# Layer 1's attention probabilities: turned in pairs through block transposes and a DRAM scratch, beside wider weight splits, scaling on ScalarE and smaller buffers

## The chip, the core and the metric

The program runs on one core of a Trainium2 chip. Time is the device time of one execution in microseconds (us), and what is compared is the median of several runs. The engines named below are TensorE (PE in the profile, with its weight loads as PEld), VectorE (DVE), ScalarE (ACT), GpSimd (POOL) and SyncE (SP, which here issues DMAs).

## The reference, cut to what matters

Two decoder layers on 256 tokens of width 2048, batch 1, all in float32. Layer 0 mixes tokens by block-sparse attention, which for 256 keys in one block is causal attention with 16 heads of 128; layer 1 by multi-head latent attention. Each is followed by a gated MLP of width 5632 with a causal convolution. The change is in layer 1's attention, and the order of a few small operations in layer 0 goes with it:

```python
def mla_attention(h, pos, wq_a, g_qa, wq_b, wkv_a, g_kva, wkv_b, g_qn, g_kn, g_qr, g_kr, wo):
    cq = rms_norm(h @ wq_a, g_qa)
    q = (cq @ wq_b).reshape(B, S, H, NOPE + RD)          # 16 heads, 128 + 64
    q_nope = rms_norm(q[..., :NOPE], g_qn)
    q_rope = rope(rms_norm(q[..., NOPE:], g_qr), pos, RD)
    kv_a = h @ wkv_a
    ckv = rms_norm(kv_a[..., :MLA_KV_RANK], g_kva)
    k_rope = rope(rms_norm(kv_a[..., MLA_KV_RANK:], g_kr)[:, :, None, :], pos, RD)[:, :, 0]
    kv = (ckv @ wkv_b).reshape(B, S, H, NOPE + VD)
    k_nope = rms_norm(kv[..., :NOPE], g_kn)
    v = kv[..., NOPE:]
    def block(i, qn, qr):                                # 128 queries
        s = (einsum('bqhd,bkhd->bhqk', qn, k_nope) + einsum('bqhr,bkr->bhqk', qr, k_rope)) * scale
        s = where(pos[None, :] <= q_pos[:, None], s, NEG_INF)
        p = softmax(s, axis=-1)
        return einsum('bhqk,bkhd->bqhd', p, v)
    o = sweep_query_blocks(block, (q_nope, q_rope), Q_BLOCK)
    return o.reshape(B, S, H * VD) @ wo
```

## The kernel before

All weights stream from HBM once. They come in **pieces** of 128 x 512 float32 (16 pieces of 128 x 576 for `mla_wkv_a`), two pieces to a **unit** of 512 KB, 740 units in all. `Stream.load` starts a unit's DMA on SyncE's queue into one of `AHEAD_UNITS` = 6 raw buffers. `Stream.split` (L113) turns a piece w into two float32r parts: ScalarE copies `whi` (rounded), VectorE subtracts to get `wlo` = w - whi. Each product of TensorE is made of three: hi x hi, hi x lo, lo x hi. The two parts of a piece stand in one of 5 buffers of a pool; a piece is split up to 4 pieces before its use.

The work of TensorE is a list `quanta`, one entry for each piece: `tok_major` (6 products with 512 moving columns, the activations as weights) or `feat_major` (12 products with 256 moving columns, the piece as weights). The loop at the end of `trunk` (L1343) writes out, for each quantum q, `ws.split(q + 4)`, then the quantum's products, then what was planned for q: `first_in` entries (`leading`) ahead of `at` entries (`side`). So every engine's program is in the order of the quanta, and a number such as q0 + 9 in a plan is a place in that order, not a time.

Layer 0's attention works in groups g of four heads, 48 quanta each; two heads form a `Pair` (L665): their scores are made, exponentiated and normalised in one tile `s` of 6 x 128 columns; `cross` (L677) turns 32 x 32 blocks on VectorE and writes them to DRAM with four DMAs, `crossed` (L681) reads them back with one, and `turned` (L684) splits what arrived into hi and lo parts. `values` then multiplies by v, and `parted` splits the output into `oT`.

Layer 1's attention has 12 quanta to a group (four pieces each of keys, queries and values; group 0 has four more for the rotary part). A head (class `Head`, L548) is on its own: `scores` (L555), `biased` (mask and row minimum, VectorE), `exps` (ScalarE), `normal` (L614, one reciprocal and two multiplications on VectorE), `turn` (L619, three 128 x 128 transposes on TensorE into PSUM), `turned` (L625, two copies on ScalarE and a subtraction on VectorE), `values` (L634) and `parted` (L645). Head i of a group has its scores at q0 = q_q + 11 + 3i, its transposes at q0 + 6 and its values at q0 + 9 (8 for the fourth), where q_q is the group's last quantum of queries (in group 0, of keys). A group's transposes, values and scores of three different heads so fall in one quantum. Two PSUM banks (`ps_sc`) serve scores and outputs in turn, two (`ps_tp`) the transposes, four the accumulators.

At the start, `Stream.begin` (L94) issues the first six units and x in alternation. `n1.sums` (quantum 29) needs the sum of 16 squares, one VectorE addition each (L346) in quanta 17 to 28; `signed_gains` (L816, 6 small VectorE operations) stands at quantum 26 and `gained_moba` (L827, 3 each) at 27 and 28.

Of the kernel before, what the change touches and what calls it, by code (L numbers as in the profile page):

```python
# [41 lines left out]

AHEAD_UNITS = 6
AHEAD_PIECES = 4

SINGLE_UNITS = 8
# [23 lines left out]
class Stream:  # L70

    def __init__(self, nc, raw_pool, part_pool, units, starts):
        self.starts = starts
# [18 lines left out]
    def begin(self, load_x):  # L94

        ends = {1: 3, 3: 5, 5: 8, 8: 12, 11: 16}
        load_x(0, 1)
        at = 1  # L100
        for u in range(AHEAD_UNITS):
            src, k, n = self.units[u]
            self.raw[u] = t = self.raw_pool.tile([P, 2 * 512], F32, name="raw")
            for i in range(k):
                queue = self.nc.scalar if u == i == 0 else self.nc.sync
                queue.dma_start(t[:, i * n : (i + 1) * n], src[:, i * n : (i + 1) * n])
                end = ends.get(u * k + i, at)
                if end > at:
                    load_x(at, end)
                    at = end  # L110
        self.loaded = AHEAD_UNITS

    def split(self, upto):  # L113
        while self.split_to < min(upto, len(self.pieces)):
            i = self.split_to
            u, j, n = self.pieces[i]
            self.load(u + AHEAD_UNITS)
            w = self.raw[u][:, j * n : (j + 1) * n]
            b, c = self.starts(u, j)
            hi = self.part_pool.tile([P, 512 + ROOM], F32R, name="whi")[:, b : b + max(n, 512)]  # L120
            lo = self.part_pool.tile([P, 512 + ROOM], F32R, name="wlo")[:, c : c + max(n, 512)]
            if i == 0:
                self.nc.vector.tensor_copy(hi[:, :n], w)
            else:
                self.nc.scalar.copy(hi[:, :n], w)  # L125
            self.nc.vector.tensor_tensor(  # L126
                lo[:, :n], w, hi[:, :n].bitcast(F32), op=ALU.subtract
            )
            self.parts[i] = (hi, lo, n)
            self.split_to += 1  # L130

# [5 lines left out]
def trunk(ctx: ExitStack, tc: tile.TileContext, a, out):  # L137
# [33 lines left out]
    units += grouped("mla_wqr", 1, 0)  # L171
    units += units_of("mla_wkv_a", 2 * KVN)
    for g in range(4):
        names = ("mla_wkn", "mla_wqn", "mla_wv") if g else ("mla_wqn", "mla_wqr", "mla_wkn", "mla_wv")
        for name in names:
            units += grouped(name, 1, 1 if name == "mla_wqr" else g)
    units += units_of("mla_wo")
    units += units_of("ffn_gu1")
# [7 lines left out]
    assert len(units) == 740  # L186
    ws = Stream(nc, raw_pool, part_pool, units, starts)

# [8 lines left out]

    zeros = const.tile([P, 512], BF16, name="zeros")
    nc.vector.memset(zeros, 0.0)
# [221 lines left out]
    class Heads:  # L421
# [22 lines left out]
        def squared(self, t):  # L444

            if self.gain is not None:
                if t == 0:
                    self.blk = att_pool.tile([P, NT, 4 * P], F32, name="blk", bufs=1)
                sq = self.blk[:, t]
            else:  # L450
                sq = att_pool.tile([P, 16 * 32], F32, name="sq" if self.dh == P else "ro2", bufs=2)
            nc.scalar.activation(sq, self.x[:, t].rearrange("p n d -> p (n d)"), AF.Square)
# [35 lines left out]
        def rotate(self, t, stages=range(4)):  # L488
# [11 lines left out]
            def part(name):  # L500
                r = att_pool.tile([P, n * rot], F32, name=name, bufs=2)
                return r.rearrange("p (n r) -> p n r", n=n)
# [45 lines left out]
    class Head:  # L548
# [34 lines left out]
        def biased(self):  # L583
            if self.pair:
                self.s_first, self.s_second = self.pair.scores_of(self.i % 2)
            else:
                self.s = att_pool.tile([P, 3 * P], F32, name="s", bufs=3)
                self.s_first, self.s_second = self.s[:, :P], self.s[:, P:]
# [25 lines left out]
        def normal(self):  # L614
            nc.vector.reciprocal(self.st[:, 4:6], self.st[:, 2:4])
            for k, x in enumerate((self.s_first, self.s_second)):
                nc.vector.tensor_scalar(x, x, self.st[:, 4 + k : 5 + k], None, op0=ALU.mult)

# [6 lines left out]
        def turned(self):  # L625

            pT = att_pool.tile([P, 2, S], F32R, name="pT", bufs=2)
            self.pT1 = att_pool.tile([P, P], F32, name="pT1", bufs=2)
            self.pT = hi, lo = pT[:, 0], pT[:, 1]
# [3 lines left out]

        def values(self):  # L634
            o = ps_sc.tile([P, 512], F32, name="sc")
            if self.pair:
                self.pT, self.pT1 = self.pair.turned_of(self.i % 2)
            v = self.v()
            vs = slice(self.i * P, (self.i + 1) * P)
            v0, v1 = v  # L640
            three(o[:, :S], v0[:, 0, vs], v0[:, 1, vs], self.pT[0], self.pT[1], True, False)
            mm(o[:, P:S], v1[:, vs], self.pT1, start=False, stop=True)  # L642
            self.o = o
# [21 lines left out]
    class Pair:  # L665
# [31 lines left out]

        def plan(self, heads, q, q_values):
            for hd in heads:
                at(q, hd.scores)  # L700
                at(q, hd.biased)
            for hd in heads:
                at(q + 1, hd.exps)
            for hd in heads:
                at(q + 2, hd.normal)
            at(q + 3, self.cross)
            at(q + 5, self.crossed)
            first_in(q_values - 2, 1, self.turned)
            for hd in heads:
                first_in(q_values, 0, hd.values)  # L710
                first_in(q_values, 0, hd.parted)

# [338 lines left out]
    def kva_squares(half):  # L1051
# [4 lines left out]
        for t in range(NT):  # L1056
            for k, lo, hi in cols:
                junk = att_pool.tile([P, 512], F32, name="kvjunk", tag="ro1", bufs=2)
                nc.vector.tensor_tensor_reduce(
# [238 lines left out]
    for g in range(4):  # L1298
        for kind in "kqv" if g else "qrkv":
# [10 lines left out]
            else:  # L1310
# [10 lines left out]
                plan_latent(q, hs, ("qT" if kind == "q" else "kT", g), with_gain(put, c), *steps)  # L1321
        for i in range(4):
            hd = Head(
                4 * g + i, lambda g=g: env["qT", g], lambda g=g: env["kT", g], lambda g=g: env["v", g],
                i, lambda: env["oT"],
                rope=lambda h=4 * (g % 2) + 2 * (i % 2) + i // 2: (env["qrT"][:, h], env["kr"]),
            )
            q0 = q_q + 11 + 3 * i
            last = g == i == 3
            hd.plan(q0, q0 + (7 if last else 8 if i == 3 else 9), q0 + 5 if last else None)  # L1330

# [132 lines left out]
```

## Time and profile before

| | us |
|---|---|
| median of 3 runs | 2073.11 (2072.75 to 2073.43) |
| the profiled execution: its own time | 2073.38 |
| the profiled execution: span, first to last instruction | 2071.1 |
| TensorE busy in the span | 2065.1 |
| VectorE busy | 1420.7 |
| ScalarE busy | 1157.7 |
| mean granted TensorE clock | 1.000 of full speed |

The span is what the profile's views divide up; 2.3 us of the execution lie around it. Matmuls are pipelined, so the duration of one (about 276 ns for 256 columns) is longer than the distance from its start to the next one's start; costs on TensorE are read from starts. VectorE's and ScalarE's instructions overlap their neighbours by a little as well, so that sums of durations come out above busy time.

### The profile page before, as it was taken

What the parts mean: (1) busy time and instruction counts of PE and PEld (TensorE: products, weight loads), DVE (VectorE), ACT (ScalarE), POOL (GpSimd) and SP (SyncE); (2) the same over time, 40 slices, a digit from 0 to 9 for tenths busy, and PEclk for the clock granted to TensorE, in tenths of its full rate; (3) what the DMA queues carried; (4) which work ended last, traced back from release to release, by engine and by line L of the source; (5) the groups of instructions that cost most, each with busy time, mean ns of one, the idle gap of its engine ahead of it and who ended that gap; (6) DMA issues with size and microseconds to landing.
All of it is one profiled execution on the core that took longest, in us unless ns stands there. A gap on an engine that the chain in (4) does not pass through costs nothing.

```text
span 2071.1 us, 42736 instructions
## 1 busy us (share of the span) xinstructions
PE 2065.1 (100%) x16630; PEld 1999.5 (97%) x16630; DVE 1420.7 (69%) x2781; ACT 1157.7 (56%) x2244; POOL 47.1 (2%) x38
## 2 busy tenths in 40 slices
PE   9999999999999999999999999999999999999999
PEld 7888899999999999999999889999999999999999
DVE  7877777766676666655556897767666766665554
ACT  6656666555555555555555786655555555544443
POOL 0000000000000000000000110000000000000000
PEclk9999999999999999999999999999999999999999
DMA  7777776555555555555554533555555555556563
GB/s 272 234 246 224 231 233 208 194 193 195 194 196 192 194 195 196 197 196 192 194 196 154 193 128 131 196 189 192 194 194 198 191 194 194 198 201 200 196 212 123
DMA packets 123931, 406.47 MB, mean 196 GB/s; under 512 B 14528, under 2 KB 25280, under 8 KB 123728
## 3 DMA queue, kind: packets, MB, share of 16 engines
q1 hardware_dynamic: 123408, 403.38, 58.0%
q8 instruction: 130, 2.13, 0.4%
q14 instruction: 73, 0.60, 0.1%
q10 hardware_dynamic: 288, 0.33, 0.1%
q0 software_dynamic: 32, 0.04, 0.0%
HBM read 394.25 MB, written 9.44 MB: 195 GB/s over the span
## 4 chain that ended last, share of the span: by engine, by line
PE 98%; DVE 1%; DMA 1%; ACT 0%; issue 0%; SPq 0%; DVEq 0%; ACTq 0%
PE acc L301 26%; PE acc L303 26%; PE acc L302 26%; PE acc L275 16%; PE tp L536 0%; PE sc L544 0%; PE sc L545 0%; PE sc L543 0%; PE sc L642 0%; PE sc L565 0%; DMA xT<-in_xT 0%; DVE wlo L126 0%; PE tp L622 0%; ACT whi L125 0%; DMA raw<-in_moba_wk 0%; PE sc L581 0%
## 5 line engine op out<-in xcount | busy, mean ns | idle before, releaser
L126 DVE TENSOR_TENSOR wlo<-raw,whi 128x512 fp32r<-128x512 f32 (+1 forms) x1464 | 998.7, 689 | 377.2 <-ACT whi L125 373.6
L125 ACT CAST whi<-raw 128x512 fp32r<-128x512 f32 (+1 forms) x1463 | 870.8, 619 | 459.9 <-PE acc L302 216.9
L301 PE MATMUL acc<-h,whi 128*128 128x256 f32 x2880 | 795.4, 276 | 0.0
L303 PE MATMUL acc<-h,wlo 128*128 128x256 f32 x2880 | 794.9, 276 | 0.0
L302 PE MATMUL acc<-h,whi 128*128 128x256 f32 x2880 | 794.9, 276 | 0.0
L302 PEld LDWEIGHTS acc<-h,whi 128*128 128x128 f32 x2880 | 540.7, 188 | 0.0
L301 PEld LDWEIGHTS acc<-h,whi 128*128 128x128 f32 x2880 | 540.6, 188 | 0.0
L303 PEld LDWEIGHTS acc<-h,wlo 128*128 128x128 f32 x2880 | 540.6, 188 | 0.0
L301 PE MATMUL acc<-a,whi 128*128 128x256 f32 x1408 | 388.6, 276 | 0.0
L302 PE MATMUL acc<-a,whi 128*128 128x256 f32 x1408 | 388.6, 276 | 0.0
L303 PE MATMUL acc<-a,wlo 128*128 128x256 f32 x1408 | 388.6, 276 | 0.0
L275 PE MATMUL acc<-whi,h 128*128 128x512 f32 (+1 forms) x896 | 266.0, 377 | 0.5 <-ACT h L323 0.5
L301 PEld LDWEIGHTS acc<-a,whi 128*128 128x128 f32 x1408 | 264.3, 188 | 0.0
L302 PEld LDWEIGHTS acc<-a,whi 128*128 128x128 f32 x1408 | 264.3, 188 | 0.0
L303 PEld LDWEIGHTS acc<-a,wlo 128*128 128x128 f32 x1408 | 264.3, 188 | 0.0
L275 PEld LDWEIGHTS acc<-whi,h 128*128 128x128 f32 x896 | 164.8, 188 | 31.2 <-ACT h L323 1.0
L275 PE MATMUL acc<-wlo,h 128*128 128x512 f32 (+1 forms) x448 | 168.5, 376 | 0.2 <-DVE wlo L126 0.2
L301 PE MATMUL acc<-oT,whi 128*128 128x256 f32 x512 | 142.6, 278 | 0.0
L303 PE MATMUL acc<-oT,wlo 128*128 128x256 f32 x512 | 141.6, 277 | 0.0
L302 PE MATMUL acc<-oT,whi 128*128 128x256 f32 x512 | 141.5, 276 | 0.0
L949 DVE TENSOR_TENSOR g<-acc,rstd_b 128x256 f32<-128x256 f32 x88 | 37.5, 426 | 126.8 <-PE acc L303 123.9
L956 ACT ACTIVATE c<-g,par 128x256 f32<-128x256 f32 x88 | 53.1, 603 | 108.0 <-DVE g L949 108.0
(204 smaller groups left out, 1618.7 us busy)
## 6 DMA issues: line engine op xcount, KB each, us to landing
raw<-in_ffn_gu SPq DMA_DIRECT2D x352, 512.0 KB, 4.4
raw<-in_ffn_down SPq DMA_DIRECT2D x176, 512.0 KB, 4.5
raw<-in_moba_wk SPq DMA_DIRECT2D x32, 512.0 KB, 5.5
raw<-in_moba_wv SPq DMA_DIRECT2D x32, 512.0 KB, 5.2
raw<-in_moba_wo SPq DMA_DIRECT2D x32, 512.0 KB, 4.5
raw<-in_mla_wo SPq DMA_DIRECT2D x32, 512.0 KB, 3.7
raw<-in_moba_wq SPq DMA_DIRECT2D x24, 512.0 KB, 5.4
raw<-in_mla_wkv_a SPq DMA_DIRECT2D x16, 288.0 KB, 3.0
```

Source lines behind the costliest of these rows:

```text
L125: self.nc.scalar.copy(hi[:, :n], w)
L126: self.nc.vector.tensor_tensor(lo[:, :n], w, hi[:, :n].bitcast(F32), op=ALU.subtract)
L275: mm(state["acc"][t][:, :n], src[:, kt, c : c + P], (t_lo if part == 1 else t_hi)[:, :n], start=kt == 0 and part == 0, stop=kt == k_last a ...
L301: mm(o, w_hi, src[:, kt, :S], start=first and k == 0, stop=False, skip_group_check=True)
L302: mm(o, w_hi, src[:, kt, S:], start=False, stop=False, skip_group_check=True)
L303: mm(o, w_lo, src[:, kt, :S], start=False, stop=kt == k_last, skip_group_check=True)
L949: nc.vector.tensor_tensor(self.g[:, 2:], self.gate["acc"][:, :S], self.norm.rstd_b, op=ALU.mult)
L956: nc.scalar.activation(self.c, self.g[:, 2:], AF.Identity, bias=par[:, cb : cb + 1], scale=self.cw(2))
```

## The change

1. Layer 1: heads 0 to 13 go in pairs through `Pair`, as layer 0's do: no transposes on TensorE for these 14; VectorE block transposes, four DMAs out and one in for a pair instead. In a pair the second head follows one quantum behind the first (`apart=1`), exponentials come two quanta behind the scores (`wait=2`), `cross` stands at q0 + 5, `crossed` at q0 + 7, `turned` at q0 + 12 and both heads' values at q0 + 14, with q0 = q_q + 11 + 3b for pair b. So the scores of a group stand at 11, 12, 14 and 15 behind q_q, where they stood at 11, 14, 17 and 20. Heads 14 and 15 stay as they were.
2. In `normal`, layer 1's two multiplications become ScalarE activations (`AF.Copy` with a scale per row).
3. A pair's values, in both layers, go into the two halves of one PSUM bank, and `parted` handles both heads in one copy and one subtraction of 512 columns.
4. The split parts stand in 3 buffers of two pieces each; for the units of layer 1's heads (26 units, 52 pieces) both pieces of a unit are split by one ScalarE copy and one VectorE subtraction of 1024 columns.
5. Raw buffers: 5 in place of 6; the last part of x is issued behind piece 9 in place of piece 11.
6. `signed_gains` moves from quantum 26 to 30, `gained_moba` from 27 and 28 to 31 and 33.
7. Several tiles share space (tags) with others, among them the squares, the rotary products, `kvjunk`, `zeros` and the probabilities of heads 14 and 15.

```diff
-AHEAD_UNITS = 6
+AHEAD_UNITS = 5
 AHEAD_PIECES = 4
+PAIRS = 3
...
-        ends = {1: 3, 3: 5, 5: 8, 8: 12, 11: 16}
+        ends = {1: 3, 3: 5, 5: 8, 8: 12, 9: 16}
...
-            w = self.raw[u][:, j * n : (j + 1) * n]
-            b, c = self.starts(u, j)
-            hi = self.part_pool.tile([P, 512 + ROOM], F32R, name="whi")[:, b : b + max(n, 512)]
-            lo = self.part_pool.tile([P, 512 + ROOM], F32R, name="wlo")[:, c : c + max(n, 512)]
+            if i % 2 == 0:
+                self.pair = [
+                    self.part_pool.tile([P, 2, 512 + ROOM], F32R, name=name) for name in ("whi", "wlo")
+                ]
+            k = 2 if u in self.double else 1
+            w = self.raw[u][:, j * n : (j + k) * n].rearrange("p (k n) -> p k n", k=k)
+            hi, lo = (
+                tile[:, i % 2 : i % 2 + k, at : at + n] for tile, at in zip(self.pair, self.starts(u, j))
+            )
             if i == 0:
-                self.nc.vector.tensor_copy(hi[:, :n], w)
+                self.nc.vector.tensor_copy(hi, w)
             else:
-                self.nc.scalar.copy(hi[:, :n], w)
...
+            self.nc.vector.tensor_tensor(lo, w, hi.bitcast(F32), op=ALU.subtract)
+            for m in range(k):
+                self.parts[i + m] = (hi[:, m], lo[:, m], n)
+            self.split_to += k
...
-    part_pool = ctx.enter_context(tc.tile_pool(name="parts", bufs=AHEAD_PIECES + 1))
+    part_pool = ctx.enter_context(tc.tile_pool(name="parts", bufs=PAIRS))
...
             for k, x in enumerate((self.s_first, self.s_second)):
-                nc.vector.tensor_scalar(x, x, self.st[:, 4 + k : 5 + k], None, op0=ALU.mult)
+                r = self.st[:, 4 + k : 5 + k]
+                if self.rope is None:
+                    nc.vector.tensor_scalar(x, x, r, None, op0=ALU.mult)
+                else:
+                    nc.scalar.activation(x, x, AF.Copy, scale=r)
...
+        def values(self, heads):
+            self.o = ps_sc.tile([P, 512], F32, name="sc")
+            for t, hd in enumerate(heads):
+                hd.pT, hd.pT1 = self.turned_of(t)
+                hd.values(self.o[:, t * S : (t + 1) * S])
+
+        def parted(self, heads):
+            h, oT = heads[0].h, heads[0].oT()
+            hi, lo = oT[:, h : h + 2, :S], oT[:, h : h + 2, S:]
+            o = self.o.rearrange("p (t s) -> p t s", t=2)
+            nc.scalar.copy(hi, o)
+            nc.vector.tensor_tensor(lo, o, hi.bitcast(F32), op=ALU.subtract)
+
+        def plan(self, heads, q, q_values, apart=0, wait=1):
+            for t, hd in enumerate(heads):
+                at(q + apart * t, hd.scores)
+                at(q + apart * t, hd.biased)
+                at(q + wait + apart * t, hd.exps)
+                at(q + wait + 1 + apart * t, hd.normal)
+            at(q + wait + 2 + apart, self.cross)
+            at(q + wait + 4 + apart, self.crossed)
             first_in(q_values - 2, 1, self.turned)
+            first_in(q_values, 0, self.values, heads)
+            first_in(q_values, 0, self.parted, heads)
...
-    at(26, signed_gains)
+    at(30, signed_gains)
     for i in range(2):
-        at(27 + i, gained_moba, i)
+        at(31 + 2 * i, gained_moba, i)
...
+        for b in range(2):
+            pair = Pair() if g < 3 or b == 0 else None
+            heads = [
+                Head(
+                    4 * g + i, lambda g=g: env["qT", g], lambda g=g: env["kT", g], lambda g=g: env["v", g],
+                    i, lambda: env["oT"], pair=pair,
+                    rope=lambda h=4 * (g % 2) + 2 * (i % 2) + i // 2: (env["qrT"][:, h], env["kr"]),
+                )
+                for i in (2 * b, 2 * b + 1)
+            ]
+            if pair:
+                q0 = q_q + 11 + 3 * b
+                pair.plan(heads, q0, q0 + 14, apart=1, wait=2)
+                continue
+            for i, hd in enumerate(heads):
+                q0 = q_q + 17 + 3 * i
+                hd.plan(q0, q0 + (9, 7)[i], q0 + 5 if i else None)
```

More of the change, by code (lines that the diff above doesn't have):

```diff
@@ L70, with __init__ @@
 class Stream:
-    def __init__(self, nc, raw_pool, part_pool, units, starts):
-        self.starts = starts
+    def __init__(self, nc, raw_pool, part_pool, units, starts, double):
+        self.starts, self.double = starts, double
         self.nc, self.raw_pool, self.part_pool = nc, raw_pool, part_pool
@@ L172, in trunk @@
     units += units_of("mla_wkv_a", 2 * KVN)
+    u_heads = len(units)
     for g in range(4):
@@ L176, in trunk @@
             units += grouped(name, 1, 1 if name == "mla_wqr" else g)
+    double = range(u_heads, len(units))
     units += units_of("mla_wo")
@@ L186, in trunk @@
     assert len(units) == 740
-    ws = Stream(nc, raw_pool, part_pool, units, starts)
+    ws = Stream(nc, raw_pool, part_pool, units, starts, double)
     att = ExitStack()
@@ L196, in trunk @@
     nc.gpsimd.memset(ones, 1.0)
-    zeros = const.tile([P, 512], BF16, name="zeros")
+    zeros = att_pool.tile([P, 512], BF16, name="zeros", tag="pT1", bufs=1)
     nc.vector.memset(zeros, 0.0)
@@ L450, in squared @@
             else:
-                sq = att_pool.tile([P, 16 * 32], F32, name="sq" if self.dh == P else "ro2", bufs=2)
+                tag, bufs = ("sq", 2) if self.dh == P else (("sblk", 1), ("s", 2))[t]
+                sq = att_pool.tile([P, 16 * 32], F32, name="sq", tag=tag, bufs=bufs)
             nc.scalar.activation(sq, self.x[:, t].rearrange("p n d -> p (n d)"), AF.Square)
@@ L500, in part @@
             def part(name):
-                r = att_pool.tile([P, n * rot], F32, name=name, bufs=2)
+                r = att_pool.tile([P, n * rot], F32, name=name, bufs=2 if n * rot < 512 else 1)
                 return r.rearrange("p (n r) -> p n r", n=n)
@@ L586, in biased @@
             else:
-                self.s = att_pool.tile([P, 3 * P], F32, name="s", bufs=3)
+                self.s = att_pool.tile([P, 3 * P], F32, name="s", tag="sq", bufs=2)
                 self.s_first, self.s_second = self.s[:, :P], self.s[:, P:]
@@ L625, in turned @@
         def turned(self):
-            pT = att_pool.tile([P, 2, S], F32R, name="pT", bufs=2)
-            self.pT1 = att_pool.tile([P, P], F32, name="pT1", bufs=2)
+            homes = ("sblk", "qr") if self.i == 2 else ("ro1", "ro2")
+            pT = att_pool.tile([P, 2, S], F32R, name="pT", tag=homes[0], bufs=1)
+            self.pT1 = att_pool.tile([P, P], F32, name="pT1", tag=homes[1], bufs=1)
             self.pT = hi, lo = pT[:, 0], pT[:, 1]
@@ L632, in turned, with values @@
             nc.vector.tensor_tensor(lo, self.tp[:, :S], hi.bitcast(F32), op=ALU.subtract)
[L634 to L637, printed above, removed]
+        def values(self, o=None):
+            o = ps_sc.tile([P, 512], F32, name="sc") if o is None else o
+            flags = {"skip_group_check": True} if self.pair else {}
             v = self.v()
@@ L640, in values @@
             v0, v1 = v
-            three(o[:, :S], v0[:, 0, vs], v0[:, 1, vs], self.pT[0], self.pT[1], True, False)
-            mm(o[:, P:S], v1[:, vs], self.pT1, start=False, stop=True)
+            three(o[:, :S], v0[:, 0, vs], v0[:, 1, vs], self.pT[0], self.pT[1], True, False, **flags)
+            mm(o[:, P:S], v1[:, vs], self.pT1, start=False, stop=True, **flags)
             self.o = o
@@ L696, in turned_of @@
             return (self.pT[:, 0, t], self.pT[:, 1, t]), self.pT1[:, t]
[L698 to L707, printed above, removed]
+        def values(self, heads):
[17 more added lines that the diff above has]
+            at(q + wait + 4 + apart, self.crossed)
             first_in(q_values - 2, 1, self.turned)
-            for hd in heads:
-                first_in(q_values, 0, hd.values)
-                first_in(q_values, 0, hd.parted)
+            first_in(q_values, 0, self.values, heads)
+            first_in(q_values, 0, self.parted, heads)
     n1 = Norm(C_AN, False)
@@ L1057, in kva_squares @@
             for k, lo, hi in cols:
-                junk = att_pool.tile([P, 512], F32, name="kvjunk", tag="ro1", bufs=2)
+                junk = att_pool.tile([P, 512], F32, name="kvjunk", tag="sq", bufs=2)
                 nc.vector.tensor_tensor_reduce(
@@ L1321, in trunk @@
                 plan_latent(q, hs, ("qT" if kind == "q" else "kT", g), with_gain(put, c), *steps)
[L1322 to L1330, printed above, removed]
+        for b in range(2):
[15 more added lines that the diff above has]
+                hd.plan(q0, q0 + (9, 7)[i], q0 + 5 if i else None)
     n4 = Norm(C_FN + KD, True)
```

6 lines of the change are left out of this document (1 added, 5 removed).

## The prediction

> **What bounds the kernel now.** I read the page first, then busy time by windows, then who waited on TensorE, then the timeline of single engines around the places that the diff touches.
>
> ```profile
> PE 2065.1 (100%) x16630; PEld 1999.5 (97%) x16630; DVE 1420.7 (69%) x2781; ACT 1157.7 (56%) x2244; POOL 47.1 (2%) x38
> ...
> PEclk9999999999999999999999999999999999999999
> ...
> PE 98%; DVE 1%; DMA 1%; ACT 0%; issue 0%; SPq 0%; DVEq 0%; ACTq 0%
> ```
>
> TensorE is busy throughout at full clock, and 98% of the chain that ended last is its own. Time falls only if its queue gets shorter or a hole in it closes. Two windows, one in the MLP and one over two head groups of layer 1 (columns: window, length, busy time of PE, PEld, DVE, ACT, POOL, clock, DMA share, GB/s):
>
> ```profile
> 600.00:700.00 100.00, 100.00 (x885) 100.00 (x884) 69.29 (x129) 53.42 (x102) 0.00 (x0) 1.00 0.57 194
> 1190.40:1242.50 52.10, 52.09 (x312) 45.30 (x311) 50.55 (x137) 44.72 (x119) 7.79 (x4) 1.00 0.36 126
> ```
>
> In the MLP a matmul leaves every 113 ns (100 us by 885), so a piece of 12 lasts 1.36 us. In layer 1's heads TensorE still has no hole, but VectorE is busy 97% and ScalarE 86%: that is where a shorter TensorE queue could meet another engine. The whole list of who waited on TensorE has one entry ahead of the first weights and these:
>
> ```profile
> PE tp L370 <- DVE nacc L346: 0.7, 1, 0.7
> PE acc L275 <- ACT h L323: 0.5, 1, 0.5
> PE acc L275 <- DVE wlo L126: 0.2, 1, 0.2
> ```
>
> All lie in the first 50 us.
>
> **Transposes leave TensorE.** One head's quantum on TensorE before, and behind it the seam between a pair's two heads in layer 0, which already runs as the new code will (columns: start, length, operation, count):
>
> ```profile
> 1214.42 0.28 PE L545 MATMUL sc<-pT,rparts 128*128 128x256 f32 x1
> 1214.54 0.39 PE L642 MATMUL sc<-pT,room 128*128 128x128 f32 x2
> 1214.76 0.49 PE L622 MATMUL tp<-ident,s 128*128 128x128 f32 x3
> 1215.09 0.39 PE L565 MATMUL sc<-room 128*128 128x128 f32 x2
> 1215.23 0.36 PE L543 MATMUL sc<-rparts 128*128 128x256 f32 x1
> 1215.44 0.28 PE L544 MATMUL sc<-rparts 128*128 128x256 f32 x1
> ...
> 108.22 0.39 PE L642 MATMUL sc<-pT,v 128*128 128x128 f32 x2
> 108.36 0.36 PE L543 MATMUL sc<-pT,v 128*128 128x256 f32 x1
> ```
>
> From start to start the three transposes take 1215.09 - 1214.76 = 0.33 us, 0.11 each. Fourteen heads lose 42: **4.6 us**. The new plan also tears scores and values apart, so there are about ten more seams between float32 and float32r products. A seam makes the first float32r product last 0.21 (1215.23 to 1215.44) where its like takes 0.12 (1214.42 to 1214.54); but the float32 pair ahead of it then takes 0.14 (108.22 to 108.36) where with more float32 behind it it takes 0.22. Plus 0.09, minus 0.08: ten seams cost 0.1 us, left out. The matmul count else stays.
>
> [...] The sum goes by starts.
>
> **What takes their place.** Costs on the other engines, from the two-group window by shape, and the block transpose from its own line (columns: count | busy, mean ns | idle before):
>
> ```profile
> L125 ACT CAST whi<-raw 128x512 fp32r<-128x512 f32 x26 | 16.2, 630 | 0.0
> L609 ACT ACTIVATE s<-s,sst 128x256 f32<-128x256 f32 x8 | 4.1, 507 | 0.0
> L735 ACT ACTIVATE room<-tp,par 128x256 f32<-128x256 f32 x7 | 3.4, 490 | 0.0
> L609 ACT ACTIVATE s<-s,sst 128x128 f32<-128x128 f32 x8 | 3.3, 415 | 1.7 <-DVE sst L601 1.6
> L630 ACT CAST pT<-tp 128x256 fp32r<-128x256 f32 x8 | 3.0, 374 | 0.2 <-PE tp L622 0.2
> L648 ACT CAST oT<-sc 128x256 fp32r<-128x256 f32 x7 | 2.6, 371 | 1.3 <-PE sc L642 1.3
> L631 ACT COPY pT<-tp 128x128 f32<-128x128 f32 x8 | 2.2, 276 | 0.0
> ...
> L126 DVE TENSOR_TENSOR wlo<-raw,whi 128x512 fp32r<-128x512 f32 x25 | 17.1, 685 | 0.8 <-ACT whi L125 0.7
> L617 DVE TENSOR_SCALAR s<-s,sst 128x256 f32<-128x256 f32 x8 | 2.8, 348 | 0.0
> L617 DVE TENSOR_SCALAR s<-s,sst 128x128 f32<-128x128 f32 x8 | 2.3, 287 | 0.3
> ...
> L410 DVE STREAM_TRANSPOSE sblk<-s x8: 970/972/972, 92.9 to 305.5; 128x768 f32<-128x768 f32 x8
> ```
>
> *ScalarE, for a group of four heads.* The scaling activation isn't in this trace. For 256 columns it lies between 374 (a plain cast) and 507 (the exponential); I take 490, the scaled copy. For 128, between 276 and 415; 400. Four heads: 4 x 0.89 = +3.6. A 1024-wide copy lies between 630 and 2 x 630; 256 more columns cost 630 - 374 = 256, so 630 + 512 = 1.14 against 1.26: six of them, -0.7. A pair's `turned` is 630 and 374 against 2 x (374 + 276), -0.3, two pairs -0.6; its `parted` 630 against 742, -0.2. Net **+2.1 us on 44.7 / 2 = 22.4**: 24.5.
>
> *VectorE.* Scaling, -4 x 0.635 = -2.5; transposes, +2 x 0.97 = +1.9; wider instructions a little less (bounds 0 and -0.9 for six subtractions): net about -1, 24.3 of 25.3 now.
>
> TensorE's group shrinks from 26.05 by 12 x 0.11 = 1.3 to 24.7. So ScalarE comes within 0.2 us of it. Sums of durations overstate (the ScalarE rows overlap by about 0.1 us each), so the true room is larger, some 1 us. I cost this at **nothing**, its cover being the parts split up to four pieces ahead; bounds 0 and +4 (first rival).
>
> [...]
>
> **The way through DRAM.** The issue list's last column is the median time to landing:
>
> ```profile
> there<-sblk SPq DMA_DIRECT2D x32, 96.0 KB, 2.3
> s<-there SPq DMA_DIRECT2D x8, 384.0 KB, 4.5
> raw<-in_moba_wk SPq DMA_DIRECT2D x32, 512.0 KB, 5.5
> ```
>
> Seven pairs add 35 DMAs to SP's queue. Transposes 1.0, four issues about 1.8, landings 2.3 and 4.5: 9.6 us, and the plan leaves seven quanta of 24.7 / 12 = 2.06 us, 14.4, from `cross` to `turned`, and two more to the values. Hidden, with 4.8 to spare. While SP waits for `there` to land, weight loads queue behind it; while ScalarE waits at `turned`, the next splits and exponentials do. The loads have the cover of five units, ten pieces: 13.6 us less the 5.4 of four pieces ahead leaves 8.2 against a landing of 5.5. Cost nothing; with late loads in layer 0, up to 1 us. Wider splits make a pair's first piece ready some 1.0 us later and its second a quantum earlier: within the lead, nothing. The five buffers, the earlier x, shared space and pair-wise `parted` in layer 0 have the same answer: nothing.
>
> **The start.** TensorE's hole and VectorE's work ahead of it:
>
> ```profile
> 47.96 0.39 PE L275 MATMUL acc<-whi,h 128*128 128x512 f32 x1
> 49.08 0.58 PE L370 MATMUL tp<-ones,nacc 128*128 128x1 f32 x4 [0.73 <-DVE nacc L346]
> ...
> 44.99 0.18 DVE L823 TENSOR_SCALAR gains<-gains 128x32 f32<-128x32 f32 x1
> ...
> 45.50 0.42 DVE L346 TENSOR_TENSOR nacc<-nacc,nsq 128x256 f32<-128x256 f32 x1
> ...
> 46.44 0.22 DVE L835 TENSOR_TENSOR mtab<-tab,gains 128x64 f32<-128x64 f32 x1
> ...
> 46.78 0.42 DVE L346 TENSOR_TENSOR nacc<-nacc,nsq 128x256 f32<-128x256 f32 x1
> ...
> 47.71 0.22 DVE L835 TENSOR_TENSOR mtab<-tab,gains 128x64 f32<-128x64 f32 x1
> ...
> 48.05 0.88 DVE L346 TENSOR_TENSOR nacc<-nacc,nsq 128x256 f32<-128x256 f32 x2
> ...
> 72.98 0.48 PE L275 MATMUL acc<-wlo,h 128*128 128x512 f32 x1
> ```
>
> The last product before the sums would free TensorE at 47.96 + 0.23; they start at 49.08: a hole of 0.89 us. The moved operations take 0.51 + 0.34 + 0.34 = 1.19 us from ahead of the last addition, which then ends at 47.7 instead of 48.9, so the hole closes. What is late next: of the moved work the first two parts fall where VectorE waits for GpSimd and ScalarE, but the last, 0.34 us at quantum 33, lands in a stretch where `wlo` arrives just in time (at 72.98 a product already lasts 0.48 against 0.39). I give 0.34 back: **-0.55 us** (bounds -0.9 and 0).
>
> **Sum.** -4.6 - 0.55 = -5.1 us. The profiled execution (span 2071.1, 2.3 around it, 2073.4) would take 2068.3; the median of the runs shown is 0.3 lower, so **2068.0 us**, 0.25% faster.
>
> **Rivals.**
> - *ScalarE becomes the bound in the heads.* For: 24.5 of 24.7 by sums, and being in order it also waits (the two-group window leaves it 7.4 us idle). Against: those are mostly waits of an engine that is ahead, and they shrink when it falls behind. If 1 us a group is lost in 3.5 groups, 3 to 4 us of the gain go: 2071.3.
> - *The transposes gave TensorE no time*, since it would wait for `wlo` from the 97% VectorE instead. Against: no wait on TensorE there. Only the start is left: 2072.5.
> - *A transpose costs its full record.* 42 x 0.275 + 0.55 = 12.1: 2061.0. [...]
> - *The other side: slower weight reading.* Two pieces share a tile, and every pool behind it moves. Equal products don't all run alike: in the first fence 0.12 us against 0.113 in the MLP. There are 14,400 products at L301 to L303; if half of them ran 2 ns slower, +14.4 - 5.1: 2082.4. It decides from 0.64 ns on the average product (5.1 + 4.15 over 14,400). Against: a buffer was 576 columns before, and the second half of a tile begins 576 columns in, so distances between pieces stay.
>
> **How the numbers follow.** About 0.2% (4.15 us, beyond 2069.0) is what a measurement of this kernel can tell from no change. Forecast 0.55 (its own range 2067.2 to 2069.2), ScalarE bound 0.22, nothing from the transposes 0.10, full record 0.03, slower reading 0.10. Faster: 0.51 + 0.02 + 0.03 = 0.56; slower 0.10; the rest, 0.34, within. The range takes in the forecast and the two rivals that stay below 2073: 2066.8 to 2072.5; the last two, 0.13, are left out.
>
> **What would show it.** Right: L622 left with 6 records; MLP windows still 885 matmuls in 100 us; the hole ahead of L370 gone, TensorE delayed by up to 0.4 us until 75 us; a head group of 24.7 us with ScalarE near 95%; no wait on TensorE behind 80 us. Wrong: TensorE waiting for `wlo`, `rparts` or `pT` at 1160 to 1290, or fewer than 885 matmuls in a window of the MLP.

## The result, and the profile after

| | before | after |
|---|---|---|
| median, us | 2073.1 (2072.75 to 2073.43) | **2094.78** (2094.42 to 2095.25, 4 runs) |
| span of the profiled execution | 2071.1 | 2092.2 |
| TensorE waiting for others behind 80 us | nothing | 17.6 in six entries |

The ratio is 1.0104 (95% interval 1.0092 to 1.0117): the changed kernel is 21.7 us **slower**, where 5.1 us less were forecast. Busy time and the chain that ended last, from the page of after:

```profile
PE 2069.2 (99%) x16588; PEld 1998.8 (96%) x16588; DVE 1401.8 (67%) x2708; ACT 1129.5 (54%) x2221; POOL 49.3 (2%) x38
...
PE 95%; ACT 2%; DVE 2%; issue 1%; DMA 0%; SPq 0%; DVEq 0%; ACTq 0%
```

TensorE has 42 instructions less, as meant, and VectorE and ScalarE are both busy for *less* time than before. Yet TensorE's share of the chain has fallen from 98 to 95%, in favour of two engines whose work fell.

Where? I compared the start of each piece's first product in the two traces. From piece 54 to piece 840 after is ahead by a constant 0.43 us; from piece 896 (1315 us) to the end it is behind by a constant 21.22. The whole loss lies between: layer 1's heads take 136.67 us where they took 115.02. The MLP window reads as before, 885 products in 100 us, so slower weight reading is out:

```profile
520.00:620.00 100.00, 100.00 (x885) 100.00 (x884) 69.95 (x130) 52.47 (x102) 0.00 (x0) 1.00 0.57 195
```

The window over the heads, before and after (busy PE, PEld, DVE, ACT, POOL, clock, DMA share, GB/s):

```profile
1170.00:1340.00 170.00, 169.99 (x1258) 159.36 (x1257) 145.13 (x360) 125.16 (x305) 16.23 (x8) 1.00 0.44 151
```

```profile
1170.00:1340.00 170.00, 152.47 (x1027) 137.35 (x1026) 124.61 (x269) 118.61 (x269) 17.32 (x8) 0.97 0.50 156
```

TensorE is idle for 17.5 us and its clock is no longer full, while VectorE (125 of 170) and ScalarE (119) are *less* busy than before (the window holds less of the program too, 1027 products for 1258). A bound by load would show one of them nearly full. Who waited for whom in after (us in total, times, longest), on TensorE in the whole span, then on ScalarE and on VectorE between 1178 and 1322 us:

```profile
PE tp L544 <- DVE qk L491: 6.0, 3, 2.4
PE acc L282 <- ACT whi L131: 3.9, 2, 2.4
PE tp L544 <- DVE rparts L764: 3.8, 3, 1.3
PE acc L282 <- DVE wlo L132: 1.7, 3, 0.8
PE acc L308 <- ACT whi L131: 1.2, 2, 0.9
PE sc L209 <- DVE zeros L206: 1.2, 1, 1.2
PE acc L310 <- DVE wlo L132: 1.2, 3, 0.8
PE acc L282 <- ACT h L330: 0.7, 1, 0.7
```

```profile
ACT s L629 <- DVE sst L623: 19.4, 16, 3.0
```

```profile
DVE wlo L132 <- ACT whi L131: 16.9, 12, 2.3
DVE rparts L764 <- ACT room L757: 11.8, 9, 2.1
```

Before, the same two waits of VectorE were these, in the same stretch, and ScalarE had no reciprocal to wait for:

```profile
DVE wlo L126 <- ACT whi L125: 4.4, 8, 1.0
DVE rparts L742 <- ACT room L735: 0.5, 2, 0.3
```

On TensorE the wait L370 of before is gone, two entries are the start's (L206, L330), and the other six are new, 17.6 us between 1178 and 1322 (0.2 of L132's 1.7 belong to the start): TensorE stands for weights' parts and for scaled or copied queries and keys. The other lists show why: the scaling on ScalarE (L629) stands 19.4 us for VectorE's reciprocal (L623), and VectorE stands 28.7 us for ScalarE's copies, where it stood 4.9. One such stretch in the timeline of after, ScalarE, VectorE and TensorE (start, length, operation, in brackets the idle time ahead and its releaser):

```profile
1236.22 1.03 ACT L131 CAST whi<-raw 128x1024 fp32r<-128x1024 f32 x1
1237.28 1.23 DVE L132 TENSOR_TENSOR wlo<-raw,whi 128x1024 fp32r<-128x1024 f32 x1 [2.15 <-ACT whi L131]
...
1238.43 0.16 DVE L623 RECIPROCAL sst<-sst 128x2 f32<-128x2 f32 x1
...
1238.68 0.80 ACT L629 ACTIVATE s<-s,sst 128x128 f32<-128x128 f32 x2 [1.43 <-DVE sst L623]
...
1239.95 0.46 ACT L757 ACTIVATE room<-tp,par 128x256 f32<-128x256 f32 x1
...
1240.45 0.75 DVE L764 SCALAR_TENSOR_TENSOR rparts<-tp,par,rparts 128x512 fp32r<-128x512 f32 x1 [1.86 <-ACT room L757]
...
1241.25 0.33 PE L544 MATMUL tp<-ident,qk 128*128 128x128 f32 x1 [1.24 <-DVE rparts L764]
```

Read it down: while ScalarE copies, VectorE is idle (2.15); while VectorE subtracts and takes the reciprocal, ScalarE is idle (1.43); then VectorE again (1.86). Work that ran side by side now runs in turn. The split for pieces to come (two at a time here, so in every second quantum) is written out *ahead* of the scaling in a quantum, so VectorE's reciprocal stands behind `wlo`, which waits for ScalarE's `whi`; and ScalarE's scaling, which waits for that reciprocal, has the key copies and the next `whi` behind it.

### The profile page after: what moved, and what is told of

It reads as the page before. It is cut to its first block, busy times and chain, and to the rows that moved or that the text cites. A ratio compares the mean times of both kernels' runs of the same rounds, so it can differ in the third digit from the quotient of the medians.

```text
span 2092.2 us, 41595 instructions
## 1 busy us (share of the span) xinstructions
PE 2069.2 (99%) x16588; PEld 1998.8 (96%) x16588; DVE 1401.8 (67%) x2708; ACT 1129.5 (54%) x2221; POOL 49.3 (2%) x38
## 4 chain that ended last, share of the span: by engine, by line
PE 95%; ACT 2%; DVE 2%; issue 1%; DMA 0%; SPq 0%; DVEq 0%; ACTq 0%
PE acc L310 26%; PE acc L308 26%; PE acc L309 26%; PE acc L282 16%; ACT s L629 0%; ACT s L617 0%; DVE wlo L132 0%; ACT whi L131 0%; PE tp L544 0%; PE sc L553 0%; PE sc L552 0%; PE sc L551 0%; PE sc L654 0%; DMA xT<-in_xT 0%; PE sc L573 0%
## 5 line engine op out<-in xcount | busy, mean ns | idle before, releaser
L132 DVE TENSOR_TENSOR wlo<-raw,whi 128x512 fp32r<-128x512 f32 (+2 forms) x1438 | 981.6, 698 | 392.5 <-ACT whi L131 389.5
L131 ACT CAST whi<-raw 128x512 fp32r<-128x512 f32 (+2 forms) x1437 | 832.5, 625 | 407.4 <-PE acc L309 265.3
L971 DVE TENSOR_TENSOR g<-acc,rstd_b 128x256 f32<-128x256 f32 x88 | 37.5, 426 | 126.6 <-PE acc L310 123.7
```

The lines of the kernel that those rows point to most:

```text
L131: self.nc.scalar.copy(hi, w)
L132: self.nc.vector.tensor_tensor(lo, w, hi.bitcast(F32), op=ALU.subtract)
L971: nc.vector.tensor_tensor(self.g[:, 2:], self.gate["acc"][:, :S], self.norm.rstd_b, op=ALU.mult)
```

## The experiments

Layer 1's heads are measured as the time from piece 840 to piece 896 against before (115.02 us, by starts of TensorE's products). "Clock" is the time lost to a lower granted clock, from windows of 2 us (sum of 2 us times what is missing to 1.00). Both are read from each kernel's profiled execution, and the clock is not the same in all: of e5's ten executions five list 1.000 (2072.5 to 2073.2 us, the profiled one among them) and five 0.999 (2074.1 to 2074.8), e7's divide in much the same way, six and four, and e10's profiled one is of the two among its ten at 0.999. The lost time is not simply part of the loss either; e2 below shows why. The intervals of e5, e7, e9, e11 and e14 include 1.

| kernel | median us | ratio, interval | heads | clock |
|---|---|---|---|---|
| after | 2094.78 | 1.0104 (1.0092-1.0117) | +21.7 | 5.1 |
| e1 scaling back on VectorE | 2083.72 | 1.0050 (1.0033-1.0067) | +11.5 | 5.2 |
| e2 splits one by one | 2095.31 | 1.0107 (1.0092-1.0122) | +23.3 | 11.9 |
| e3 scaling a quantum late | 2078.90 | 1.0028 (1.0017-1.0039) | +6.6 | 3.4 |
| e4 before + scaling on ScalarE | 2089.70 | 1.0080 (1.0065-1.0095) | +16.6 | 1.7 |
| e5 = e3 + output copies late | 2073.69 | 1.0004 (0.9994-1.0013) | +0.5 | 0 |
| e6 = e3 + splits one by one | 2081.60 | 1.0041 (1.0027-1.0055) | +10.0 | 5.1 |
| e7 = e3 + heads two quanta apart | 2074.07 | 1.0005 (0.9996-1.0014) | +0.7 | 0 |
| e8 before, transposes left out | 2068.27 | 0.9978 (0.9969-0.9987) | -4.8 | 0 |
| e9 = e5 and e7 | 2072.94 | 1.0000 (0.9992-1.0009) | +0.7 | 0 |
| e10 = e9, scaling on VectorE | 2075.85 | 1.0014 (1.0005-1.0023) | +4.9 | 1.7 |
| e11 = e5, scaling two quanta late | 2071.61 | 0.9993 (0.9984-1.0002) | -0.8 | 0 |
| e12 = e4, scaling a quantum late | 2076.22 | 1.0016 (1.0007-1.0025) | +3.3 | 0 |
| e13 = e11, queries' scaling earlier | **2070.55** | 0.9988 (0.9979-0.9997) | -2.9 | 0 |
| e14 = e9, queries' scaling earlier | 2071.81 | 0.9994 (0.9985-1.0003) | -0.7 | 0 |

### First: which of the edits, and load or order

e1 and e2 undo one edit of after; e4 makes one edit in before; e3 leaves all work where it is and moves only the place of the scaling in the order.

e1, in `normal` of after:

```diff
-                if self.rope is None:
-                    nc.vector.tensor_scalar(x, x, r, None, op0=ALU.mult)
-                else:
-                    nc.scalar.activation(x, x, AF.Copy, scale=r)
+                nc.vector.tensor_scalar(x, x, r, None, op0=ALU.mult)
```

e2, in after:

```diff
-    double = range(u_heads, len(units))
+    double = range(0)
```

e3, in `Pair.plan` of after; `inverse` is the reciprocal of `normal`, by itself:

```diff
-                at(q + wait + 1 + apart * t, hd.normal)
-            at(q + wait + 2 + apart, self.cross)
-            at(q + wait + 4 + apart, self.crossed)
+                if hd.rope:
+                    at(q + wait + 1 + apart * t, hd.inverse)
+                at(q + wait + 1 + bool(hd.rope) + apart * t, hd.normal)
+            q_cross = q + wait + 2 + apart + bool(heads[0].rope)
+            at(q_cross, self.cross)
+            at(q_cross + 2, self.crossed)
```

e4, in `normal` of before:

```diff
-                nc.vector.tensor_scalar(x, x, self.st[:, 4 + k : 5 + k], None, op0=ALU.mult)
+                r = self.st[:, 4 + k : 5 + k]
+                if self.rope is None:
+                    nc.vector.tensor_scalar(x, x, r, None, op0=ALU.mult)
+                else:
+                    nc.scalar.activation(x, x, AF.Copy, scale=r)
```

> The changed kernel with layer 1's scaling back on VectorE, all else as changed. Handover theory (ScalarE stands at the scaling until VectorE's reciprocal, which is queued behind a subtraction that itself waits for ScalarE): the 19.4 us that ScalarE waited for the reciprocal go, TensorE's waits in layer 1 mostly with them, and the time falls from 2094.8 to 2069 to 2076. Load theory (ScalarE simply has too much to do): 11 us of scaling leave ScalarE, the time falls about as far, 2070 to 2078; this run alone doesn't tell the two apart. Wide splits as the cause: little, 2088 to 2095. Crowded schedule or the DRAM trip as the cause: 2088 to 2095.

> The changed kernel with every piece split on its own, the scaling still on ScalarE. Handover theory: each handover gets shorter by the 0.4 us of the copy and the 0.5 us of the subtraction, some 14 of them count, 2082 to 2090. Load theory: two narrow copies cost ScalarE 0.1 us more than a wide one, so no gain, 2093 to 2098. Wide splits as the cause: the loss goes, 2069 to 2076.

> The changed kernel with the reciprocal left at its quantum and the two scalings on ScalarE one quantum later (block transposes and the way back from DRAM one quantum later as well); ScalarE's load is the same. Handover theory: ScalarE no longer stands at the scaling, and most of the loss goes, 2070 to 2080. Load theory: no gain, 2091 to 2098. Wide splits as the cause: 2088 to 2096.

> The kernel before with the scaling on ScalarE as its only edit; transposes, narrow splits and the wide spacing of heads stay. Handover theory: ScalarE stands at the reciprocal once a head here as well, in front of a shorter subtraction and with room of three quanta between heads: 2075 to 2085. Load theory: ScalarE goes from 86% to about 95%, the same as in the changed kernel: 2080 to 2092. Wide splits or the crowded schedule as the cause: 2072 to 2075.

e3 lies where order as the cause put it, and far from the load theory: with the same activations on ScalarE, 15.9 us come back. e4 shows that the scaling on ScalarE costs 16.6 us in the old kernel without any other edit, more than order as the cause had allowed (2075 to 2085) and inside the load theory's range. e1 missed both: with the scaling back, 10.6 us stay, of which e10 below, with two more edits of the order, takes back 7.9. e2 missed what order as the cause expected (2082 to 2090) and lies in the load theory's range. Its window:

```profile
1170.00:1340.00 170.00, 155.51 (x1013) 138.52 (x1012) 125.07 (x285) 119.34 (x286) 16.22 (x8) 0.93 0.52 157
```

TensorE's idle time is 14.5 us where it was 17.5, and the mean clock 0.93 where it was 0.97. That doesn't show that shorter splits shortened the standing, for the executions of each of the two kernels differ as much in clock among themselves. After lists a clock of 0.998 in 2094.42 us and of 0.993 in 2095.25; e2 lists 0.998 in 2094.66 and 0.993 in 2095.38, and the two that were profiled are one of 0.998 (after) and one of 0.994 (e2). At the same clock the two kernels take the same time. And 0.005 of clock, some 10 us, lengthen after by only 0.8 us; my estimate, from the two windows (17.5 us idle at 0.97, 14.5 at 0.93), is that a slower TensorE had less standing left there.

e12 decides between load and order without the pairs: e4 with its scaling one quantum behind the reciprocal.

```diff
-            at(q + 2 + late + (late and q_turn == q + 6), self.normal)
+            if late:
+                at(q + 2 + late + (late and q_turn == q + 6), self.inverse)
+            at(q + 2 + 2 * late + (late and q_turn == q + 6), self.normal)
```

> e4 (the kernel before with its scalings on ScalarE as the only edit, 2089.70 us), with the scaling one product behind its reciprocal; ScalarE's and VectorE's work is the same as in e4. Handover theory: the standing in turn goes, 2073-2079 us. Load theory (ScalarE has 25 us of work in a group of 26): nothing changes, 2087-2091.

13.5 of the 16.6 us come back. ScalarE's waits for VectorE in e4, then in e12 (1150 to 1330 us), and the window of e12:

```profile
ACT s L621 <- DVE sst L615: 31.2, 16, 3.4
```

```profile
ACT s L625 <- DVE sst L615: 8.9, 8, 2.4
```

```profile
1170.00:1340.00 170.00, 168.58 (x1231) 156.11 (x1230) 135.09 (x323) 133.33 (x332) 16.22 (x8) 1.00 0.45 148
```

The same 32 activations make ScalarE wait 31.2 us in one place of the order and 8.9 one quantum later, and with the wait gone it does *more* work in the same 170 us (133.3 against 123.7 in e4) without holding TensorE. Order, not load, is the cause of most of the loss.

### Second: what e3 still lost, and what the transposes are worth

e5, in `Pair.plan` of e3 (e6 is e2's edit in e3):

```diff
-            first_in(q_values, 0, self.parted, heads)
+            first_in(q_values + bool(heads[0].rope), 0, self.parted, heads)
```

e7, in e3:

```diff
-                pair.plan(heads, q0, q0 + 14, apart=1, wait=2)
+                pair.plan(heads, q0, q0 + 14, apart=2, wait=2)
```

e8, in before:

```diff
-            nc.scalar.copy(hi, self.tp[:, :S])
-            nc.scalar.copy(self.pT1, self.tp[:, S : 3 * P])
-            nc.vector.tensor_tensor(lo, self.tp[:, :S], hi.bitcast(F32), op=ALU.subtract)
+            nc.scalar.copy(hi, self.s[:, :S])
+            nc.scalar.copy(self.pT1, self.s[:, S : 3 * P])
+            nc.vector.tensor_tensor(lo, self.s[:, :S], hi.bitcast(F32), op=ALU.subtract)
...
-            first_in(q_turn, 1, self.turn)
```

> As e3 (2078.90 us), with the two copies of a pair's outputs out of PSUM put one product later than the products of the values, instead of right behind them. Three theories of the 5.8 us that e3 still lost. Handover theory: the rest is again engines waiting in turn: ScalarE stands at the output copy for TensorE's products of the values (11.4 us in e3), VectorE at the output's remainder behind it, and the latent's scaling, for which TensorE waits 5.5 us, is queued behind that remainder; with the copy one product later it finds its input there, and the time falls to 2071-2075 us. Crowding theory (four heads' scores within five products make VectorE late): nothing changes, 2077-2080. Wide-splits theory (a subtract of 1.22 us at a time): nothing changes, 2077-2080.

> As e3 (2078.90 us), with every piece of the weights split alone (two copies of 0.62 us and two subtracts of 0.68 us in place of one of 1.04 and one of 1.22). Wide-splits theory: 2071-2075 us. Handover theory: no less than 2076, up to 2082, since twice as many copies and subtracts wait for each other. Crowding theory: 2077-2081.

> As e3 (2078.90 us), with the two heads of a pair two products apart instead of one (scores of a group at products 11, 13, 14, 16 instead of 11, 12, 14, 15), and the block transposes a product later. Crowding theory: VectorE's work is less bunched, 2070-2075 us. Handover theory: the waits at the output copies stay, 2076-2081. Wide-splits theory: 2077-2080.

> The kernel before with one thing left out: the 48 TensorE transposes of layer 1's probabilities. The copies that took the turned blocks out of PSUM read the unturned ones in SBUF instead, so the probabilities stay unturned. This measures the gain of the prediction's first term alone. By starts (0.11 us each): 48 x 0.11 = 5.3 us less, 2067.8 us (2067.2-2068.4). If TensorE fills with the next weight load what the transposes leave: 2072-2073.5. If a transpose costs its whole record (0.27 us): 2060. If the copies were held back by other things than the transposes, it could fall by less than 5.3, 2068.5-2071.

**e8** took 4.74 us less for 48 transposes, 0.099 us each; the trace has 4.79 between pieces 840 and 896. The prediction's first term holds (0.11), and 42 are worth 4.2 us.

**e5 and e7** each gain about 5 us, in the ranges of two different theories, so neither range proves its theory. The traces say what happened. On ScalarE, e5's edit did what it was for: the stand at the output copies fell from 11.4 us to 2.2 (to 3.7 in e7, which has no such edit). But the wait of TensorE at the end of the chain, for the scaling of the queries (L491; e5's expectation calls it the latent's), shrank from 5.5 us in e3 to only 4.7 in e5 (from TensorE's wait lists of the two, 1150 to 1330 us):

```profile
PE tp L544 <- DVE qk L491: 5.5, 3, 2.4
```

```profile
PE tp L544 <- DVE qk L491: 4.7, 3, 2.1
```

What went besides is the fall of the clock: 3.4 us lost in the profiled e3, nothing in the profiled e5 and e7. In e3 it follows a stop of TensorE (columns as in the windows above):

```profile
1229.70:1231.70 2.00, 0.15 (x3) 0.01 (x1) 1.42 (x3) 2.00 (x5) 0.00 (x0) 1.00 1.03 225
1231.70:1235.00 3.30, 3.30 (x11) 2.61 (x12) 2.99 (x5) 3.17 (x6) 0.00 (x0) 0.55 0.85 312
```

TensorE does 0.15 us of work in 2.00, and then runs at 0.55 for the next 3.30. So of the 6.1 us by which the heads of the profiled e5 are shorter, 3.4 are clock and 1.8 are waiting of TensorE (6.5 in e3, 4.7 in e5). e5's explanation by the output copies holds for ScalarE's stand and not for TensorE's wait, and e7's by crowding is not shown. **e6** came out slower than e3, by 2.7 us: more handovers and a clock loss of 5.1 us against 3.4. The wide splits are no part of the loss.

### Third: both edits, the engine, the distance

e9 has the edits of e5 and e7, e10 the same two in e1. e11, in `Pair.plan` of e5:

```diff
-                at(q + wait + 1 + bool(hd.rope) + apart * t, hd.normal)
-            q_cross = q + wait + 2 + apart + bool(heads[0].rope)
+                at(q + wait + 1 + 2 * bool(hd.rope) + apart * t, hd.normal)
+            q_cross = q + wait + 2 + apart + 2 * bool(heads[0].rope)
```

> e5 and e7 together: after, with the scaling one product behind its reciprocal, the output copies one product behind the values, and the two heads of a pair two products apart. If the two edits took away different waits, the 4.8 us that each gained over e3 (2078.90 us) add in part: 2070-2072.5 us. If both took away the same wait (one stretch in which the clock of TensorE also fell), it is as each alone: 2073-2074.5.

> As e9, but with the scaling on VectorE as in the kernel before, in the same product as the reciprocal. Handover theory: no handover at the scaling at all, and the waits at the output copies are gone too, so VectorE's longer queue is all that is left: 2069-2073 us. Load theory for VectorE (block transposes of 0.97 us and scalings on one engine are too much): 2075-2082.

> As e5 (2073.69 us), with the scaling two products behind its reciprocal instead of one. ScalarE still stood 7.0 us at the scaling for the reciprocal in e5. Handover theory: one product of 2.2 us is not always enough of a distance, two are: 2070-2073 us. If what is left in e5 is something else (the latent's scaling on VectorE, queued behind the key's remainder): 2073-2075.

e9 lies between its two cases (2072.94) and is not a sum of two gains: its eleven executions, all at a clock of 1.000, lie where those of e5 and e7 at 1.000 do (2072.5 to 2073.2, 2073.0 to 2074.2). That fits a fall of the clock which each edit takes away: over the heads the profiled e3 has two, the profiled e5, e7 and e9 have none. e10 missed order as the cause and lies in the load theory's range for VectorE. The wait list of TensorE in e10:

```profile
PE tp L544 <- DVE qk L491: 3.7, 3, 1.6
PE acc L282 <- DVE wlo L132: 1.7, 2, 1.0
PE acc L309 <- DVE oT L718: 1.3, 1, 1.3
```

All three wait for VectorE, which now has the scalings and the block transposes. So taking the scaling off VectorE does help these pairs, by 2.9 us (e10 against e9), provided that it stands far enough behind the reciprocal. e11 with two quanta of distance is 2.1 us faster than e5 (1.1 against e5's executions at a clock of 1.000).

### Fourth: the last wait

What was left in e5, e9 and e11 is the same wait, and e5's timeline shows its chain:

```profile
1226.86 0.16 DVE L623 RECIPROCAL sst<-sst 128x2 f32<-128x2 f32 x1
...
1227.12 0.80 ACT L633 ACTIVATE s<-s,sst 128x128 f32<-128x128 f32 x2
1227.83 0.67 ACT L764 ACTIVATE rparts<-tp,par 128x512 fp32r<-128x512 f32 x1
...
1228.39 0.46 ACT L764 ACTIVATE room<-tp,par 128x256 f32<-128x256 f32 x1
...
1228.89 0.75 DVE L771 SCALAR_TENSOR_TENSOR rparts<-tp,par,rparts 128x512 fp32r<-128x512 f32 x1 [1.04 <-ACT room L764]
...
1229.56 0.68 DVE L491 TENSOR_TENSOR qk<-qk,hr 128x512 f32<-128x512 f32 x1
...
1230.29 0.55 PE L544 MATMUL tp<-ident,qk 128*128 128x128 f32 x3 [1.41 <-DVE qk L491]
```

The queries' scaling L491 needs nothing of all this; it is only written behind the keys' remainder L771, which waits for ScalarE's copy, which stands behind the scaling of the probabilities. e13 and e14 move L491 one quantum ahead (for groups 1 to 3; group 0 has places of its own):

```diff
-                    "q": ((0, 1), (1, 3), 3, (5, 7), (9, 10)), "k": ((0, 0), (1, 2), 2, (5, 7), (10, 11)),
+                    "q": ((0, 1), (1, 3), 3, (5, 6), (9, 10)), "k": ((0, 0), (1, 2), 2, (5, 7), (10, 11)),
```

> As e11 (2071.61 us), with the second scaling of a group's queries on VectorE one product earlier (6 products after the queries' last piece instead of 7), where it stands ahead of the two remainders of the keys that wait for ScalarE. In-order theory of what is left: TensorE's wait of 2.1 us for that scaling goes, 2069.5-2071.0 us. If what is left has another cause (the DRAM trip, ScalarE's 5.4 us at the turned blocks, or VectorE's work as such): 2071.3-2073.

> As e9 (2072.94 us: scaling one product late, output copies one late, heads two apart), with the same edit as e13. In-order theory: TensorE waits 3.8 us in e9 for that scaling, and most of it goes, 2069.5-2071.5 us. Otherwise: 2072.5-2074.

In both the wait for L491 is gone or down to 0.4 us. e13 lies in the range of the in-order theory; e14 ends 0.3 us above it, though 3.4 us of its wait went, and where the rest stays is not shown. e13 beats both kernels: 2070.55 us, 0.12% under before (0.03 to 0.21%; it is the best of the variants, and the interval only just leaves out no change) and 24.2 us under after. It keeps the wide splits, the five raw buffers and the shared space of after, so none of these is needed to explain the loss. TensorE's wait list of e13 between 1150 and 1330 us, and two groups by window:

```profile
PE sc L551 <- ACT qk L449: 1.3, 1, 1.3
```

```profile
1208.80:1260.72 51.92, 50.64 (x341) 45.42 (x339) 47.70 (x108) 47.65 (x115) 7.61 (x4) 1.00 0.60 182
```

The one wait left is a new one. It follows a stand of ScalarE at `turned` for the DRAM trip, which in e13 has two quanta less than in after; the instructions behind it come late (timeline of e13):

```profile
1234.59 0.62 ACT L707 CAST pT<-s 128x512 fp32r<-128x512 f32 x1 [2.12 <-DMA s<-there]
...
1235.42 1.04 ACT L131 CAST whi<-raw 128x1024 fp32r<-128x1024 f32 x1
...
1236.37 1.26 ACT L449 ACTIVATE qk<-acc,cscale 128x512 f32<-128x512 f32 x2
...
1237.06 0.36 PE L551 MATMUL sc<-pT,rparts 128*128 128x256 f32 x1 [1.28 <-ACT qk L449]
```

The heads gain 2.9 us, the transposes' 4.2 less this hole of 1.3.

## Why the prediction was wrong, point by point

- **The failed step: "I cost this at nothing, its cover being the parts split up to four pieces ahead; bounds 0 and +4."** The scaling on ScalarE cost 16.6 us alone (e4). I priced it as a *load*, 24.5 of 24.7 us a group, and asked whether ScalarE had room. As a load it does: in e13's two groups ScalarE is busy 47.65 of 51.92 us and TensorE loses 1.3. What I left out is that moving the scaling makes a *wait* where none was: before, reciprocal and multiplications followed each other on VectorE. I never named what stands behind that wait on ScalarE, nor that the reciprocal stands in VectorE's queue behind a `wlo` that waits for ScalarE. The four pieces ahead were no cover, since the splits are themselves among the instructions that stand.
- *"Those are mostly waits of an engine that is ahead, and they shrink when it falls behind"* (the first rival) did not hold here, where two engines wait for each other: VectorE's two largest waits for ScalarE grew from 4.9 us to 28.7, and with ScalarE's 19.4 for VectorE they come to 48 us in after.
- *The order of the pairs* has no term in the sum: scores one quantum apart, and one copy for two heads' outputs right behind their values, priced as load alone (-0.2). With the scaling back on VectorE (e1) 10.6 us of loss stay, and e10's two edits of that order take back 7.9. What each of the two is worth there was not run, so this part of the cause is shown less closely than the scaling.
- *The transposes, -4.6 us:* right; 0.099 each by e8, so -4.2.
- *The start, -0.55 us:* right. Between pieces 24 and 54 after gains 0.61 us: the hole closes, and 0.35 is given back, much as said (0.34). L377 was L370; it now starts 0.23 us behind the last product:

```profile
48.15 0.39 PE L282 MATMUL acc<-whi,h 128*128 128x512 f32 x1
...
48.38 0.50 PE L377 MATMUL tp<-ones,nacc 128*128 128x1 f32 x4
```

- *Block transposes and DRAM trip hidden:* no wait for the trip in the list of after, so right there, but 4.8 us was the whole reserve: two quanta less, in e13, and ScalarE waits for it (2.12 us in the timeline above). In e10, where VectorE has the block transposes and the scaling, TensorE waits 6.7 us for VectorE; how much of it is the transposes' is not shown.
- *ScalarE's durations:* two groups of e13 by shape:

```profile
L131 ACT CAST whi<-raw 128x1024 fp32r<-128x1024 f32 x7 | 7.4, 1055 | 0.0
L633 ACT ACTIVATE s<-s,sst 128x256 f32<-128x256 f32 x8 | 4.1, 512 | 0.0
...
L633 ACT ACTIVATE s<-s,sst 128x128 f32<-128x128 f32 x8 | 3.3, 418 | 0.1
```

  0.93 us a head against 0.89, and 1.06 against 1.14 for the wide copy: the sizes were right, and did not matter. ScalarE gained 3.0 us in two groups (44.63 in 52.80 before, 47.65 in 51.92), less than the 4.2 of the forecast.
- *Wider splits nothing:* right (e2, e6: narrow is no faster).
- *Rivals:* ScalarE as the bound was the nearest, but by load, and with 3 to 4 us, where the miss is 26.8. The "other side" was slower weight reading, which the MLP window excludes. A transpose's full record, 0.275 us, is the mean of L622's 48 records in before; by e8 a transpose was worth 0.099. The handover was not among them. The list "what would show it" did name it: TensorE waiting for `wlo` and `rparts` in this stretch.
- *The engine of the multiplication:* with VectorE the time was shorter in e1 (11.1 us under after) and in before (16.6 us under e4), with ScalarE in e9 (2.9 us under e10). The durations of the instructions (0.93 us a head on ScalarE in e13, 0.635 on VectorE in before) didn't decide; the neighbours in the queue did.

## What to carry to other kernels

When an operation moves to another engine, count the new wait before the load: write down what stands ahead of its producer in the one queue and what stands behind the operation in the other, and see whether the two queues now wait for each other. If they do, put a stage of the schedule between producer and consumer; here that was worth 13.5 and 15.9 us at the same work. And read idle time of *both* engines with the bottleneck's waits: two engines at some 70% that held up a third were, here, standing in turn.

## What the runs showed of the hardware

Stretches at half clock follow stops of TensorE in these traces, in after three of them, each at the end of a group's stops. Around the first, in steps of 3.41 us (columns as above):

```profile
1202.46:1205.87 3.41, 1.93 (x6) 1.05 (x6) 1.30 (x2) 1.98 (x5) 0.00 (x0) 1.00 0.63 210
1205.87:1209.28 3.41, 0.67 (x5) 0.48 (x5) 3.27 (x5) 3.41 (x8) 0.00 (x0) 1.00 0.21 44
1209.28:1212.70 3.42, 3.42 (x13) 2.73 (x11) 3.40 (x5) 2.26 (x5) 0.00 (x0) 0.50 0.88 260
1212.70:1216.11 3.41, 3.41 (x22) 2.98 (x21) 2.42 (x7) 2.65 (x6) 0.87 (x1) 1.00 0.92 324
```

The third row is at 0.50 from end to end. The low stretches over the heads last one, two or three such steps (3.41 us each in after; 6.84, 3.40, 3.40 and 10.24 in e2, by the windows of 2 us), and in after, e1, e3 and e6 they begin a whole number of steps apart (34.1 us in after, ten steps; 30.7 in the others, nine).

In the step ahead of a fall TensorE was busy (as the profile models busy time) for 0.67, 0.39 and 0.59 us of 3.41 in after, and for 1.56 and 0.99 in e3 (46% and 29%, by its timeline); it was not wholly idle in any of the five. After's steps with 1.71, 1.93 and 1.94 us (50 to 57%; from 1233.18, 1202.46 and 1236.59 on) were followed by steps at full clock, and one of e2 with 1.7 to 1.9 us (the step that ends at 1207.24) by one at half. What decides there is not shown. The profiled e5 and e7, where TensorE waits 4.7 and 4.5 us (6.5 in e3), have no low stretch there.

Such a step loses 1.7 us of full clock (half of 3.41). e5's executions at 0.999, which by my estimate is one such step in a mean over 2071 us, take some 1.6 us longer than those at 1.000 (2074.4 against 2072.8 in the mean). In after a lower clock costs far less, as told at e2.
